# Second parts of split weights on VectorE, a ring of 2 MB slots for the second mixture, and a reordered chain in the first

## The chip, the cores and the metric

The kernel runs on one core of a Trainium2 chip as one program. The metric is the device time of one execution in microseconds; less is better. Four compute engines work side by side, each in its own order: TensorE (PE in the profile; its weight loads are PEld), VectorE (DVE), ScalarE (ACT) and GpSimd (POOL). SyncE (SP) issues most of the DMAs, which 16 DMA engines carry out.

## The reference

Two transformer blocks on 512 tokens of width 1024, in fp32. The first block: a mixer (mLSTM heads and a multi-scale pool), cross attention to a memory of 256 rows, and a mixture of 16 experts of width 256, two for each token. The second: a modulated Hyena convolution in its FFT form, and a mixture in which each of 16 experts of width 2048 chooses its 64 tokens. Cut to what matters here:

```python
z = x @ w_in                                   # mixer: q, k, v, o, u, gates
mixed = jnp.concatenate([h, pm], axis=-1); return mixed @ w_out
# first mixture: scores -> top 2 of the best group -> tokens by expert
hb = jax.nn.silu(xb @ w_gate[ei]) * (xb @ w_up[ei]); return hb @ w_down[ei]
# second mixture (expert choice): cap = 2 * 512 / 16 = 64
gate, idx = lax.top_k(jnp.swapaxes(aff, 1, 2), cap); xe = h[bidx, idx]
he = jax.nn.silu(xe @ w1) * (xe @ w3)
ye = (he @ w2) * gate; return zeros.at[idx].add(ye)
```

The weights of the second mixture are 402.65 MB, two thirds of all that the kernel reads.

## The kernel before

The stages follow each other: mixer and filters (two generators that are interleaved, so that TensorE alternates between them), output projection (`mix_out`), attention with the modulation vectors (`macc`), first mixture (`moe1`), its sum and layer norm (`combine`), the convolution (`hyena_first`, `hyena`, columns c of 256 or 512), the second router (`route2`) and the second mixture (`moe2`). A list scheduler sets each engine's order inside a stage; buffers come from pools whose slots rotate. The big pool has seven slots, the PSUM tags two or three buffers each.

A matmul of `mm` (lines 215 to 222) on operands of the class `Sp` is three matmuls in a shorter form, high x high, high x low and low x high (L218, L219, L220). `split` (L224) makes the parts: ScalarE copies the high one (L228), and another engine subtracts it to get the low one (L231), GpSimd unless the call names VectorE. `load_w` stages 512 KB of weights and splits them. The mixer's `proj` (L613) does not split: it multiplies x and the weights `wp` in full precision (L622, two instructions in the trace for each matmul). `wx` and `wh` are split weights, `mixl` the low part of the mixed rows, `fs` and `fk` operands of the filters, `fo` a sum of mirrored columns of the convolution (L1378), `ly` and `xr` steps of the layer norms (L308, L339, L340).

In `moe1` the logits (`plg`) go to scores, to the chosen experts (`mk`), to positions (`sv`); `lists(q)` compares the positions with 0 to 127 for four experts (`oh`, L1065), multiplies by token numbers and gates together (`pli`, L1070) and gives the index (`idx`) and the gates; `gather(e)` fetches the rows by an indirect DMA. Then for each expert: `columns` transposes the rows (`pt`, L1093) to `xe`, `up` gives `hb`, `turn` transposes it to `ht` (L1125 to L1127), and `down` multiplies by `wd` to `pye` and stores.

In `route2` VectorE finds the 64 largest of 512 by eight rounds (L1590), and `psv` turns the places. In `moe2`, `piece` issues a DMA of 1 MB (8 KB in each of 128 partitions) into one of 15 ring slots, with some of other shapes at the start. An expert takes 24 of them: `pa` and `pc` (L1682), `he`, the transposes `pht`, and `py` (L1724). Its 64 rows are multiplied by a row of the modulation (`yt`) and placed by `pcb` (L1737) with the matrix `ct`, whose 64 columns are the expert's gates, and added to `xr` (L1739). `pga` (L1661) is the gather of an expert's rows, done as a matmul.

Of the kernel before, what the change touches and what calls it, by code (L numbers as in the profile page):

```python
# [19 lines left out]
P = 128  # L20
S = 512
# [107 lines left out]
def layout(i):  # L129
# [45 lines left out]
    w1 = g["moe_w1_2"][0].reshape(E, 8, P, 4, 512).transpose(0, 3, 2, 1, 4)  # L175
    w3 = g["moe_w3_2"][0].reshape(E, 8, P, 4, 512).transpose(0, 3, 2, 1, 4)
    w13 = np.stack([w1[:, 0], w1[:, 1], w3[:, 0], w3[:, 1], w1[:, 2], w1[:, 3], w3[:, 2], w3[:, 3]], 1)
    o["w13"] = w13.reshape(E, 8, P, 2, 4, 512).transpose(0, 1, 3, 2, 4, 5)
    o["w2"] = g["moe_w2_2"][0].reshape(E, 8, 2, P, D).transpose(0, 1, 3, 2, 4)
# [24 lines left out]
class Builder:  # L204
# [379 lines left out]
    def mixer(self):  # L584
# [5 lines left out]
        x = self.big([P, 8, S], name="x")  # L590
        pg = self.psumt("pg")
        for h in range(4):
            nc.sync.dma_start(x[:, 2 * h:2 * h + 2], T["xT"][:, 2 * h:2 * h + 2])
            for k in (2 * h, 2 * h + 1):
                c = 32 * (k % 4)
                te.matmul(pg[c:c + 32], wg[:, k], x[:, k], start=k < 4, stop=k >= 4)
# [207 lines left out]
    def mix_out(self, xr, x1):  # L804

        m, mixed = self.bigsp([P, 8, S], "mix"), self.mixed
        for j in range(4):
            t = slice(j * P, (j + 1) * P)
            self.split(mixed[:, :, t], m[:, :, t], (self.nc.vector, self.nc.gpsimd)[j % 2])
# [147 lines left out]
    def moe1(self, xr, xT, xd):  # L957
# [17 lines left out]
        p = self.psumt("plg")  # L975
        for k in range(8):
            c = 32 * (k % 4)
            te.matmul(p[c:c + 32], rw[:, k], xT[:, k], start=k < 4, stop=k >= 4)
        ls = self.work(name="ls")
        act.activation(ls, p, AF.Copy)  # L980
        p = self.psumt("plt")[:, :64].rearrange("p (j e) -> p j e", e=E)
        for j in range(4):
            self.mm(p[:, j], ls[:, j * P:(j + 1) * P], sr)
        sc = sm([4, E], "sc")
        act.activation(sc, p, AF.Exp, scale=-1.0)
# [52 lines left out]
        wt = sm([4, E], "wt")  # L1038
        tt(wt, sc, mk, op=ALU.mult)
        vec.tensor_reduce(gx, wt, axis=AX.X, op=ALU.add)  # L1040
        vec.reciprocal(gx, gx)
        tt(wt, wt, gx[:, :, None].to_broadcast([P, 4, E]), op=ALU.mult)


        tg = sm([4, E, 5], "tg", BF16)
        for i in range(2):
            vec.tensor_copy(tg[:, :, :, i], row[:, :, i:i + 1].to_broadcast([P, 4, E]))
        gr = sm([4, E], "gr")
        for i in range(2, 5):
            vec.tensor_copy(tg[:, :, :, i], gr if i > 2 else wt)  # L1050
            if i < 4:
                tt(gr, gr if i > 2 else wt, tg[:, :, :, i], op=ALU.subtract)
# [8 lines left out]
        def lists(q, n=4):  # L1061
# [5 lines left out]
            p = self.psumt("pli")[:, :n * 5].rearrange("p (e c) -> p e c", c=5)  # L1067
# [3 lines left out]
            vec.tensor_reduce(idf[:, es], p[:, :, 0:2], axis=AX.X, op=ALU.add)  # L1071
            vec.tensor_copy(idx[:, es], idf[:, es])
            vec.tensor_reduce(gate[:, es], p[:, :, 2:5], axis=AX.X, op=ALU.add)
            return eq
# [22 lines left out]
        ready = lists(0)  # L1097
        for e in range(4):
            gather(e)
        cur = columns(0)  # L1100
        over = sm([4, E], "over")
# [65 lines left out]
        for e in range(E + 1):  # L1167
# [13 lines left out]
            if e < 3:  # L1181
                lists(4 * e + 4)
# [4 lines left out]
            if hb is not None:  # L1187
                down(e - 1, turn(hb))
# [313 lines left out]
    def route2(self, xr, z2, w):  # L1502
# [83 lines left out]

        m8 = self.C.tile([E, 8], F32, name="m8")
# [15 lines left out]
    def moe2(self, xr, hl, sv, aff):  # L1603
# [5 lines left out]
        m5 = self.W.tile([P, 512], F32, name="m5", tag="m5")  # L1609
# [14 lines left out]
        ring = [self.big([P, 2, 2048], name="ra") for _ in range(5)]  # L1624
        ring += [self.W.tile([P, 2, 2048], F32, name="r", tag="r", bufs=2) for _ in range(2)]
        ring = [t[:, i] for t in ring for i in range(2)]
        ring += [self.W.tile([P, 2048], F32, name="r1", tag="r1")]
        at = [0]

        spare = [self.W.tile([P, 2048], F32, name=f"s{i}", tag=f"s{i}") for i in range(2)]  # L1630
        hts = [self.W.tile([P, 1024], F32, name="ht", tag="ht"), spare[0][:, :1024]]
        xes = [self.W.tile([P, 512], F32, name="xe", tag="xe"), spare[0][:, 1024:1536]]
        cts, yts = ([spare[1][:, (2 * i + b) * 512:(2 * i + b + 1) * 512] for b in range(2)] for i in range(2))

        def piece(src, n=1):
            i, at[0] = at[0], at[0] + 1
            if i in (12, 15):

                n = 2 if i == 15 else 4
                t = [self.wide(name="r2") for _ in range(2)] if n == 2 else [m5] + [self.work(name="r4") for _ in range(3)]  # L1640
                t = [u.rearrange("p (a b) -> p a b", b=src.shape[2]) for u in t]
                h = src.shape[1] // n
                for i in range(n):
                    nc.sync.dma_start(t[i], src[:, i * h:(i + 1) * h])
                return lambda k: t[k // h][:, k % h]
            t = (ring[:13] + spare)[i] if i < 15 else ring[(i - 4) % len(ring)]
            t = t.rearrange("p (a b) -> p a b", b=src.shape[2])
            for i in range(n):
                c = slice(i * src.shape[1] // n, (i + 1) * src.shape[1] // n)
                nc.sync.dma_start(t[:, c], src[:, c])  # L1650
            return lambda k: t[:, k]

        def gather(e):
# [14 lines left out]
            xe = xes[e % 2].rearrange("p (h k s) -> p h k s", h=2, k=4)  # L1668
            act.activation(xe, pt.rearrange("p (k h s) -> p h k s", k=4, h=2), AF.Copy)
            return xe.rearrange("p h k s -> p (h k) s")  # L1670

        xs = gather(0)
        for e in range(E):
            ht = hts[e % 2].rearrange("p (k s) -> p k s", k=8)
            for hh in range(2):
                pa, pc = self.psum(name="pa"), self.psum(name="pc")
                for p, q in ((pa, 0), (pc, 2)):
                    for k2 in (0, 4):
                        w = [piece(T["w13"][e, 4 * hh + q + g, k2 // 4]) for g in range(2)]
# [94 lines left out]
```

## Time and profile before

| | |
|---|---|
| median of 3 runs (lowest, highest) | 2163.26 us (2154.15, 2169.12) |
| profiled execution | 2155.95 us |
| its span | 2154.2 us |
| TensorE busy | 1882.4 us (87%) |
| VectorE, ScalarE, GpSimd busy | 926.1, 510.3, 324.4 us |
| TensorE's mean granted clock | 0.951 |
| moved by DMA | 601.28 MB, mean 279 GB/s |

The span is the time from the first to the last instruction in the trace; 1.75 us of the profiled execution lie outside it. The granted clock is a share of 2.4 GHz: 1.00 is that level, and 0.50 is 1.2 GHz. Busy times are sums over stages that have different limits, so they are read stage by stage.

### The profile page before, as it was taken

How to read it: one execution, taken by the hardware profiler on the slowest of the kernel's cores; microseconds unless marked ns; L12 is line 12 of the kernel's file. 1: busy time of each engine (PE TensorE's matmuls, PEld its weight loads, DVE VectorE, ACT ScalarE, POOL GpSimd, SP SyncE). 2: the span in 40 equal slices, each digit the busy share in tenths (PEclk: the TensorE clock that was granted, in tenths of full speed). 3: DMA queues.
4: the chain of work that ended last, by engine and by line, in shares of the span. 5: the costliest groups of instructions: out<-in, count | busy, mean ns of one | idle time of the engine just before them, and what ended most of it. 6: DMA issues, size and time to landing. Idle time of an engine off the chain costs nothing.

```text
span 2154.2 us, 21248 instructions
## 1 busy us (share of the span) xinstructions
PE 1882.4 (87%) x8240; PEld 1009.2 (47%) x8240; DVE 926.1 (43%) x1340; ACT 510.3 (24%) x724; POOL 324.4 (15%) x208
## 2 busy tenths in 40 slices
PE   8999888989498877899786899998998888888996
PEld 2555567767265536787674233332333223332232
DVE  5666674575554548737998211111111110111113
ACT  4444223242255533443333100000000000000000
POOL 0000226310110024334653000000000000000001
PEclk9999998999699977999898899999999999999998
DMA  6443165673488861223246899999999999999995
GB/s 219 149 144 128 63 231 181 241 246 121 165 333 349 315 202 58 83 79 117 88 159 238 332 398 422 421 421 421 413 421 421 422 421 421 421 421 421 421 421 218
DMA packets 111715, 601.28 MB, mean 279 GB/s; under 512 B 14526, under 2 KB 16022, under 8 KB 58486
## 3 DMA queue, kind: packets, MB, share of 16 engines
q1 hardware_dynamic: 103478, 575.68, 68.1%
q0 software_dynamic: 3840, 13.31, 2.0%
q10 hardware_dynamic: 4288, 10.85, 1.3%
q8 instruction: 67, 1.10, 0.2%
q14 instruction: 42, 0.34, 0.1%
HBM read 577.74 MB, written 22.05 MB: 278 GB/s over the span
## 4 chain that ended last, share of the span: by engine, by line
PE 30%; DMA 19%; DVE 9%; issue 2%; POOL 1%; ACT 1%; DVEq 0%; SPq 0%; ACTq 0%; POOLq 0%
DMA ra<-in_w 12%; PE py L1724 8%; DMA r<-in_w 6%; PE pc L1682 5%; PE pa L1682 5%; PE pga L1661 2%; PE phy L218 2%; PE phy L219 1%; PE phy L220 1%; PE pcb L1737 1%; DVE wh L1415 1%; DVE fo L1378 1%; PE pht L1689 1%; DVE sp L1407 1%; DVE he L1686 1%
## 5 line engine op out<-in xcount | busy, mean ns | idle before, releaser
L1686 DVE TENSOR_TENSOR he<-he,pc 128x512 f32<-128x512 f32 x32 | 22.0, 688 | 479.7 <-PE pc L1682 452.4
L308 POOL TENSOR_TENSOR ly<-lve,mhalf 128x1 f32<-128x1 f32 x28 | 35.7, 1275 | 1068.2 <-DVE lve L320 1063.4
L231 POOL TENSOR_TENSOR wh<-w,wh 128x1024 fp32r<-128x1024 f32 x46 | 121.3, 2642 | 155.5 <-ACT wh L228 152.0
L1685 ACT ACTIVATE he<-pa 128x512 f32<-128x512 f32 x32 | 19.1, 597 | 474.8 <-PE pa L1682 468.3
L228 ACT ACTIVATE wh<-w 128x1024 fp32r<-128x1024 f32 x104 | 108.3, 1060 | 66.4 <-PE pb L220 13.7
L1727 DVE TENSOR_TENSOR s<-py,m 128x512 f32<-128x512 f32 x16 | 11.1, 691 | 227.4 <-PE py L1724 227.4
L1682 PE MATMUL pc<-ra,s 128*64 128x512 f32 x344 | 96.1, 596 | 11.6 <-DMA ra<-in_w 11.5
L1724 PE MATMUL py<-ra,ht 128*64 128x512 f32 x376 | 93.3, 595 | 0.0
L1682 PE MATMUL pc<-ra,xe 128*64 128x512 f32 x336 | 85.8, 594 | 6.6 <-DMA ra<-in_w 6.6
L1682 PE MATMUL pa<-ra,xe 128*64 128x512 f32 x336 | 86.6, 596 | 3.1 <-DMA ra<-in_w 2.4
L1682 PE MATMUL pa<-ra,s 128*64 128x512 f32 x336 | 86.1, 596 | 3.6 <-DMA ra<-in_w 3.6
L218 PE MATMUL phy<-hlh,wh 128*128 128x512 f32 (+1 forms) x240 | 87.5, 368 | 0.0
L219 PE MATMUL phy<-hll,wh 128*128 128x512 f32 (+1 forms) x240 | 86.5, 361 | 0.4 <-DVE hll L236 0.4
L220 PE MATMUL phy<-hlh,wh 128*128 128x512 f32 (+1 forms) x240 | 86.3, 360 | 0.0
L1737 PE MATMUL pcb<-s 64*128 64x512 f32 x256 | 67.7, 627 | 19.6 <-DVE s L1727 12.6
L1724 PE MATMUL py<-ra,s 128*64 128x512 f32 x312 | 81.2, 608 | 0.0
L222 PE MATMUL pye<-wd,ht 128*128 128x512 f32 x128 | 65.5, 659 | 17.3 <-ACT ht L1127 17.3
L858 DVE SCALAR_TENSOR_TENSOR macc<-wm,mc,macc 128x1024 f32<-128x1024 f32 x42 | 67.1, 1598 | 31.0 <-DMA wm<-in_modw 30.5
L1739 DVE TENSOR_TENSOR xr<-xr,pcb 128x1024 f32<-128x1024 f32 x60 | 70.6, 1218 | 20.0 <-PE pcb L1737 18.5
L231 DVE TENSOR_TENSOR wh<-w,wh 128x1024 fp32r<-128x1024 f32 x58 | 71.4, 1258 | 15.4 <-ACT wh L228 15.0
L1661 PE MATMUL pga<-hl,oh 128*64 128x512 f32 x256 | 60.3, 615 | 0.8 <-DVE oh L1656 0.8
L1682 PEld LDWEIGHTS pc<-ra,s 128*64 128x64 f32 x344 | 29.0, 137 | 65.6 <-issue 45.4
(532 smaller groups left out, 3925.7 us busy)
## 6 DMA issues: line engine op xcount, KB each, us to landing
ra<-in_w SPq DMA_DIRECT2D x254, 1024.0 KB
r<-in_w SPq DMA_DIRECT2D x125, 1024.0 KB
wm<-in_modw SPq DMA_DIRECT2D x48, 512.0 KB
w<-in_wgu SPq DMA_DIRECT2D x36, 512.0 KB
wd<-in_wd SPq DMA_DIRECT2D x16, 1024.0 KB
wg<-in_wgu SPq DMA_DIRECT2D x7, 2048.0 KB
wp<-in_wpair SPq DMA_DIRECT2D x10, 1024.0 KB
w<-in_wh SPq DMA_DIRECT2D x20, 512.0 KB
```

The source lines that it names most:

```text
L218: te.matmul(ps, a.h, b.h, start=first, stop=False, skip_group_check=skip)
L219: te.matmul(ps, a.h, b.l, start=False, stop=False, skip_group_check=skip)
L220: self.lastmm = te.matmul(ps, a.l, b.h, start=False, stop=last, skip_group_check=skip)
L222: te.matmul(ps, a, b, start=first, stop=last, skip_group_check=skip)
L228: nc.scalar.activation(d.h, f, AF.Copy)
L231: (lo_eng or nc.gpsimd).tensor_tensor(d.l, f, d.h.bitcast(F32), op=ALU.subtract)
L858: vec.scalar_tensor_tensor(acc, w, c[:, k:k + 1], acc, op0=ALU.mult, op1=ALU.add)
L1661: te.matmul(p[h * NS:(h + 1) * NS], oh[:, j], hl[:, j, h * 512:(h + 1) * 512], start=j == 0, stop=j == 3)
L1682: te.matmul(p[g * NS:(g + 1) * NS], xs[:, k2 + k], w[g](k), start=k2 + k == 0, stop=k2 + k == 7)
L1724: te.matmul(py[n * NS:(n + 1) * NS], ht[:, 4 * hh + 2 * (c % 2) + i, g * NS:(g + 1) * NS], w(i)[:, n * 512:(n + 1) * 512], start=c + i == ...
L1737: te.matmul(pb[n], ct[r, j * P:(j + 1) * P], yt[r], start=e < E - 1, stop=True)
L1739: tt(xr[:, j], xr[:, j], t.rearrange("p a b -> p (a b)"), op=ALU.add)
```

## The change

Seven edits in one.

- `split` takes VectorE where no engine is named, so the subtractions of the output projection, the attention and the convolution move there from GpSimd.
- The mixer splits x and its weights, and its projections use `mm`.
- `moe1`: the logits are made in tiles of 3 and 1 rows; `lists` multiplies by the token numbers alone, for one expert and then for three, and `weigh` makes the gates later; in the expert loop `turn` stands ahead of the next `columns`.
- `route2`: 14 matmuls on an unused PSUM tile (`pwarm`) stand after the last transposes.
- `moe2`: the weights lie in memory as pieces of 2 MB, 16 KB in each partition; `piece` fills eight slots in order, 12 pieces to an expert, and the ninth piece of all goes to other buffers by five smaller DMAs.
- `moe2`: the places of two experts are made at once (`places`); the rows of a pair stand in the two halves of the partitions, and `pcb` is done once for the pair with all 128 rows.
- There is one `ht` and one `xe` buffer, and the row of the modulation is loaded at full width.

```diff
-        (lo_eng or nc.gpsimd).tensor_tensor(d.l, f, d.h.bitcast(F32), op=ALU.subtract)
+        (lo_eng or nc.vector).tensor_tensor(d.l, f, d.h.bitcast(F32), op=ALU.subtract)
...
-        x = self.big([P, 8, S], name="x")
+        x = self.bigsp([P, 8, S], "x")
...
+            self.split(xf, x[:, 2 * h:2 * h + 2], vec)
...
-                nc.sync.dma_start(wp[0], T["wpair"][n])
+            w = self.load_w(T["wpair"][n, :, u], vec)
...
-                te.matmul(p, wp[0][:, u, k], x[:, k], start=k == 0, stop=k == 7)
+                self.mm(p, w[:, k], x[:, k], k == 0, k == 7)
...
+        for t in (slice(0, 3), slice(3, 4)):
+            n, c3 = (t.stop - t.start) * P, slice(t.start * P, t.stop * P)
+            p = self.psumt("plg")[:, :n]
...
-        ready = lists(0)
-        for e in range(4):
+        ready, oh0 = lists(0, 1)
+        gather(0)
+        _, oh1 = lists(1, 3)
+        for e in range(1, 4):
             gather(e)
         cur = columns(0)
+        wt = sm([4, E], "wt")
...
+        weigh(0, 1, oh0)
+        weigh(1, 3, oh1)
...
+            if hb is not None:
+                ht = turn(hb)
             if e + 1 < E:
                 cur = columns(e + 1)
...
-                down(e - 1, turn(hb))
+                down(e - 1, ht)
...
+        pw = self.psum(name="pwarm")
+        for i in range(14):
+            te.matmul(pw, self.ident, hl[:, 3, :512], start=True, stop=True)
...
+        slots = [self.big([P, 4096], name="ra") for _ in range(5)]
+        slots += [self.W.tile([P, 4096], F32, name="r", tag="r", bufs=3) for _ in range(3)]
...
+            t = slots[turn[0] % 8].rearrange("p (a b) -> p a b", b=1024)
+            turn[0] += 1
+            h = 4 // steps
+            for i in range(steps):
+                nc.sync.dma_start(t[:, i * h:(i + 1) * h], src[:, i * h:(i + 1) * h])
...
+            u = e % 2
+            if u == 0:
+                places(e)
...
+            for n in range(2):
+                o = (n ^ u) * NS
+                tt(yts[n][o:o + NS], py[o:o + NS], m5[o:o + NS, n * 512:(n + 1) * 512], op=ALU.mult)
+            if not u:
+                continue
```

TensorE at the start of the mixer, before: `pv` and `pqk` are projections, `psf` and `pgt` small matmuls of the filters and gates.

```order
L622 MATMUL pv<-x,wp 128x512 x8
L222 MATMUL psf<-sd,c_fw_113 64x512
L622 MATMUL pqk<-x,wp 128x512 x8
L655 MATMUL pgt<-c_ident,gn 128x64 x4
L622 MATMUL pqk<-x,wp 128x512 x4
```

The same place now:

```order
L218 MATMUL pv<-xh,wh 128x512
L219 MATMUL pv<-xl,wh 128x512
L218 MATMUL pqk<-xh,wh 128x512
L219 MATMUL pqk<-xl,wh 128x512
L222 MATMUL psf<-sd,c_fw_126 64x512
L220 MATMUL pv<-xh,wh 128x512
```

Each matmul of a projection has become three, and the first two projections are begun together.

TensorE where the first mixture's routing begins, before: the last products of attention's output, the last row's transposes, the logits.

```order
L219 MATMUL pb<-wh,oTh 128x512
L220 MATMUL pb<-wh,oTl 128x512
L360 MATMUL pt<-c_ident,xr 128x128 x8
L978 MATMUL plg<-x2T,c_rw 32x512 x8
L222 MATMUL plt<-c_sr,ls 128x16 x4
```

And now:

```order
L220 MATMUL pb<-wh,oTl 128x512
L360 MATMUL pt<-c_ident,xr 128x128 x8
L981 MATMUL plg<-x2T,c_rw 32x384 x8
L222 MATMUL plt<-c_sr,ls 128x16 x3
L981 MATMUL plg<-x2T,c_rw 32x128 x8
L222 MATMUL plt<-c_sr,ls 128x16
```

The logits of the first three tiles stand behind the transposes of the fourth, as the whole did.

ScalarE in the first mixture's expert loop, before: `wh` are copies of weights, `ye` is the scaled output.

```order
L1118 ACTIVATE hb<-pgu 128x256
L235 ACTIVATE xe<-pt 128x512
L1127 ACTIVATE ht<-pht_5578 128x256
L235 ACTIVATE xe<-pt 128x512
L1141 ACTIVATE ye<-pye,gate 128x1024
L1142 DMA yd<-ye 128x1024
L228 ACTIVATE wh<-wg 128x1024
```

And now:

```order
L1130 ACTIVATE hb<-pgu 128x256
L1139 ACTIVATE ht<-pht_5915 128x256
L235 ACTIVATE xe<-pt 128x512 x2
L1153 ACTIVATE ye<-pye,gate 128x1024
L1154 DMA yd<-ye 128x1024
L228 ACTIVATE wh<-wg 128x1024
```

The copy to `ht` has moved ahead of both copies to `xe`.

## Rows read from the trace of the kernel before

**Rows 1.** Windows: start:end, length, busy us by engine, PEclk, DMA share, GB/s

```profile
18.00:255.00 237.00, 230.04 (x740) 126.37 (x740) 153.73 (x267) 101.94 (x132) 23.90 (x36) 1.00 0.41 141
255.00:540.00 285.00, 254.01 (x1187) 194.78 (x1188) 180.35 (x210) 87.45 (x136) 87.87 (x39) 0.94 0.57 194
856.00:972.00 116.00, 105.44 (x514) 87.51 (x514) 61.15 (x107) 51.41 (x74) 41.70 (x17) 0.97 0.27 85
1228.00:1246.00 18.00, 17.16 (x85) 6.12 (x83) 1.80 (x3) 1.79 (x3) 0.00 (x0) 1.00 0.95 355
1446.00:2124.00 678.00, 611.87 (x2720) 207.02 (x2718) 98.59 (x143) 42.06 (x69) 0.00 (x0) 1.00 1.01 420
```

**Rows 2.** Timeline of TensorE in the mixer: start, us, engine, line, out<-in

```profile
26.61 7.13 PE L622 MATMUL pqk<-x,wp 128*128 128x512 f32 x16
...
60.92 0.39 PE L219 MATMUL pk<-fs,fk 128*128 128x512 f32 x1
...
62.55 0.39 PE L220 MATMUL pk<-fs,fk 128*128 128x512 f32 x1
```

**Rows 3.** Costliest groups: splits, busy us, mean ns | idle before

```profile
L228 ACT ACTIVATE wh<-w 128x1024 fp32r<-128x1024 f32 x104 | 108.3, 1060 | 66.4 <-PE pb L220 13.7
...
L231 DVE TENSOR_TENSOR wh<-w,wh 128x1024 fp32r<-128x1024 f32 x58 | 71.4, 1258 | 15.4 <-ACT wh L228 15.0
```

**Rows 4.** Groups of GpSimd from 255 to 540 us

```profile
L231 POOL TENSOR_TENSOR wh<-w,wh 128x1024 fp32r<-128x1024 f32 x24 | 63.4, 2647 | 63.4 <-ACT wh L228 63.3
...
L231 POOL TENSOR_TENSOR mixl<-mixed,mixh 128x1024 fp32r<-128x1024 f32 x2 | 5.7, 2888 | 6.6 <-ACT mixh L228 6.6
```

**Rows 5.** One line's instructions: ns min/median/max, first and last start

```profile
L858 DVE SCALAR_TENSOR_TENSOR macc<-wm,mc,macc x42: 1231/1285/3395, 295.6 to 489.3; 128x1024 f32<-128x1024 f32 x42
L1378 DVE TENSOR_TENSOR fo<-cv x8: 425/2466/2486, 854.7 to 900.4; 128x256 f32<-128x256 f32 x8
```

**Rows 6.** Waits of TensorE from 255 to 540 us: total, times, longest

```profile
PE pt L360 <- DVE xr L340: 10.8, 6, 3.8
...
PE pb L218 <- ACT wx L228: 5.5, 1, 5.5
PE pmd L866 <- DVE macc L858: 3.3, 3, 2.3
...
PE pb L219 <- DVE wx L231: 2.8, 1, 2.8
```

**Rows 7.** Timeline from 563 to 577 us

```profile
563.38 2.28 DVE L1065 TENSOR_TENSOR oh<-i128b,svb 128x2048 bf16<-128x2048 bf16 x1
567.73 0.59 PE L1070 MATMUL pli<-tg,oh 128*128 128x5 bf16 x16 [5.10 <-DVE tg L1050]
576.15 1.09 PE L1093 MATMUL pt<-c_ident,xg 128*128 128x128 f32 x4 [7.83 <-DMA xg<-xd,idx]
```

**Rows 8.** Waits of TensorE from 600 to 756 us

```profile
PE pye L222 <- ACT ht L1127: 14.8, 11, 4.3
```

**Rows 9.** Waits of TensorE from 856 to 972 us

```profile
PE pef L1325 <- DVE fo L1378: 8.8, 6, 2.0
```

**Rows 10.** Timeline of TensorE from 1190 to 1200 us

```profile
1192.10 0.73 PE L1599 MATMUL psv<-c_ident,at 16*128 16x16 f32 x4 [14.45 <-DVE at L1595]
1193.60 6.24 PE L1661 MATMUL pga<-hl,oh 128*64 128x512 f32 x16 [0.78 <-DVE oh L1656]
```

**Rows 11.** Window inside those gather matmuls

```profile
1196.00:1198.00 2.00, 2.00 (x8) 0.55 (x6) 0.00 (x0) 0.00 (x0) 0.00 (x0) 0.50 0.48 201
```

**Rows 12.** Chain that ended last: a later expert's gather

```profile
1633.04 3.43 PE pga L1661 x16
```

**Rows 13.** SyncE's queue, 1800 to 1900 and 692 to 696 us: packets, MB, share

```profile
q1 hardware_dynamic: 5771, 42.04, 101.1%
...
q1 hardware_dynamic: 84, 1.38, 80.2%
```

**Rows 14.** Timeline of TensorE from 2123 us

```profile
2123.08 9.17 PE L1724 MATMUL py<-ra,s 128*64 128x512 f32 x39
```

More of the change, by code (lines that the diff above doesn't have):

```diff
@@ L808, in mix_out @@
             t = slice(j * P, (j + 1) * P)
[L809 removed]
+            self.split(mixed[:, :, t], m[:, :, t])
         self.proj_ln(m, self.T["wmix"], xr, 0, x1)
@@ L973, in moe1 @@
         nc.sync.dma_start(yd[E * CAP:], zr)
[L975 to L983, printed above, removed]
-        sc = sm([4, E], "sc")
-        act.activation(sc, p, AF.Exp, scale=-1.0)
+        sc = sm([4, E], "sc")
+        for t in (slice(0, 3), slice(3, 4)):
+            n, c3 = (t.stop - t.start) * P, slice(t.start * P, t.stop * P)
+            p = self.psumt("plg")[:, :n]
+            for k in range(8):
+                c = 32 * (k % 4)
+                te.matmul(p[c:c + 32], rw[:, k], xT[:, k, c3], start=k < 4, stop=k >= 4)
+            ls = self.work(n, name="ls")
+            act.activation(ls, p, AF.Copy)
+            p = self.psumt("plt")[:, :64].rearrange("p (j e) -> p j e", e=E)
+            for j in range(t.start, t.stop):
+                self.mm(p[:, j], ls[:, (j - t.start) * P:(j - t.start + 1) * P], sr)
+            act.activation(sc[:, t], p[:, t], AF.Exp, scale=-1.0)
         vec.tensor_scalar(sc, sc, 1.0, None, op0=ALU.add)
@@ L1037, in moe1 @@
         vec.scalar_tensor_tensor(sv, p[:, :4], 1.0, mk, op0=ALU.add, op1=ALU.mult)
[L1038 to L1052, printed above, removed]
+        tr2 = sm([4, 2], "tr2", BF16)
+        vec.tensor_copy(tr2, row)
+        tg = sm([4, E, 3], "tg", BF16)
         idx, gate = sm([E], "idx", I32), sm([E], "gate")
@@ L1066, in lists, with weigh @@
                     svb[:, :, es, None].to_broadcast([P, 4, n, CAP]), op=ALU.is_equal)
-            p = self.psumt("pli")[:, :n * 5].rearrange("p (e c) -> p e c", c=5)
+            p = self.psumt("pli")[:, :n * 2].rearrange("p (e c) -> p e c", c=2)
+            for u in range(n):
+                for j in range(4):
+                    te.matmul(p[:, u], oh[:, j, u], tr2[:, j], start=j == 0, stop=j == 3)
+            vec.tensor_reduce(idf[:, es], p, axis=AX.X, op=ALU.add)
+            vec.tensor_copy(idx[:, es], idf[:, es])
+            return eq, oh
+        def weigh(q, n, oh):
+            p = self.psumt("plw")[:, :n * 3].rearrange("p (e c) -> p e c", c=3)
             for u in range(n):
@@ L1095, in columns @@
             return t
-        ready = lists(0)
-        for e in range(4):
+        ready, oh0 = lists(0, 1)
+        gather(0)
+        _, oh1 = lists(1, 3)
+        for e in range(1, 4):
             gather(e)
         cur = columns(0)
+        wt = sm([4, E], "wt")
+        tt(wt, sc, mk, op=ALU.mult)
+        vec.tensor_reduce(gx, wt, axis=AX.X, op=ALU.add)
+        vec.reciprocal(gx, gx)
+        tt(wt, wt, gx[:, :, None].to_broadcast([P, 4, E]), op=ALU.mult)
+        gr = sm([4, E], "gr")
+        for i in range(3):
+            vec.tensor_copy(tg[:, :, :, i], gr if i else wt)
+            if i < 2:
+                tt(gr, gr if i else wt, tg[:, :, :, i], op=ALU.subtract)
+        weigh(0, 1, oh0)
+        weigh(1, 3, oh1)
         over = sm([4, E], "over")
@@ L1632, in moe2 @@
[L1632 to L1651, printed above, removed]
+        slots = [self.big([P, 4096], name="ra") for _ in range(5)]
@@ new lines, in moe2, with piece @@
+        slots += [self.W.tile([P, 4096], F32, name="r", tag="r", bufs=3) for _ in range(3)]
+        turn = [0]
+        htb = self.W.tile([P, 1024], F32, name="ht", tag="ht")
+        xeb = self.W.tile([P, 512], F32, name="xe", tag="xe")
+        cts = [self.W.tile([P, 512], F32, name=f"ct{i}", tag=f"ct{i}") for i in range(2)]
+        yts = [self.W.tile([P, 512], F32, name=f"y{i}", tag=f"y{i}") for i in range(2)]
+        def piece(src, steps=1):
+            if turn[0] == len(slots) and slots[-1] is not None:
+                slots.append(None)
+                t = [self.wide(name="r4") for _ in range(2)] + [m5]
+                for k in range(3):
+                    nc.sync.dma_start(t[k], src[:, k])
+                t = [u[:, n * 512:(n + 1) * 512] for u in t for n in range(2)]
+                for n in range(2):
+                    t.append(yts[n])
+                    nc.sync.dma_start(yts[n], src[:, 3, n * 512:(n + 1) * 512])
+                return lambda k, n: t[2 * k + n]
+            t = slots[turn[0] % 8].rearrange("p (a b) -> p a b", b=1024)
[3 more added lines that the diff above has]
+                nc.sync.dma_start(t[:, i * h:(i + 1) * h], src[:, i * h:(i + 1) * h])
+            return lambda k, n: t[:, k, n * 512:(n + 1) * 512]
```

97 lines of the change are left out of this document (43 added, 54 removed).

## The prediction

> **What bounds the kernel now.** I read the busy time by stretch first, then in each stretch the waits of the engine that is nearest to full, then single instructions. From 18 to 255 us (mixer and filters) TensorE works 230 of 237 us at full clock, and no other engine is near: the end of this stretch is TensorE's sum of matmuls. From 255 to 540 us (output projection, attention) it idles 31 of 285 us while VectorE works 180. In the convolution from 856 to 972 us it idles 10.6 of 116. From 1446 to 2124 us the DMA engines are full at 420 GB/s, and TensorE waits for weights [rows 1]. So each microsecond saved ahead of that stream moves the stream's start, and the end with it, by as much; inside the stream only bytes and rate count.
>
> The profiled execution took 2155.95 us, 2154.2 of them in the span, 7.3 below the median of 2163.26. I sum against 2155.95 and add the 7.3 at the end.
>
> **The change part by part.**
>
> *Projections of the mixer.* A projection was 8 matmuls in full precision, 16 instructions in the trace, 7.13 us from first to last end, 16 x 0.43 = 6.9 us in a row of them. Now it is 24 matmuls of the split form. Seven of these start between 60.92 and 62.55, 0.233 us apart [rows 2], so a projection is 5.6 us: 1.3 saved, 26 us over 20 projections. All of it is on the path if the operands come in time. What it adds: 20 splits of weights and 4 of x, each an ACT copy and a VectorE subtraction of 1.26 us [rows 3]. That is 30 us, so VectorE's 154 of 237 become about 184 of some 218: cover for TensorE, but thin. x in two parts takes two slots, and the filters' operand fs has one buffer where it had two: each of eight fs then waits for the last matmul on the one before, plus about 1.06 (copy) and 1.22 (subtraction), 2.3 us, unless TensorE has a projection between; and the first projection waits for the splits of x, which I put at 3 us. If all eight gaps show, 18 + 3 of the 26 is lost. Range -26 to -5; I take **-16**, about the middle, since the order puts projections beside the filters' matmuls in some places only.
>
> *Output projection and attention.* 28 subtractions leave GpSimd: 24 of weights at 2.65 us, 2 of the mixed rows [rows 4] and 2 like them of the memory. On VectorE they cost 28 x 1.26 = 35 us. Beside a GpSimd split VectorE's own work stretches: a modulation step takes 1.285 us in the median and 3.395 at worst, the mean of the 42 is 1.598 [rows 5]; 42 x 0.31 = 13 us come back, and about 6 from the layer norms. So VectorE gets some 16 us more in a stretch where it has 105 free. What ends TensorE's waits there: the normed rows 10.8 us in six waits, the first weights of the projection 5.5 and 2.8 (behind mixed rows that GpSimd split), the modulation 3.3 [rows 6], 22.4 in all. A norm step at 1.28 for 3.4 takes about 2 from each of the longer waits, and the mixed rows' lower parts end sooner. I take **-9**, range 0 (the extra splits stand ahead of the norms on VectorE) to -16.
>
> *Routing of the first mixture.* The token lists no longer wait for the gates in three parts: the comparison of 2.28 us began at 563.38, but the list matmuls only at 567.73, after the last gate part, and the first gathered rows reached TensorE at 576.15 [rows 7]. Now the comparison is cut in 1 + 3 experts, both ahead of the index; 563.4 + 2.3 = 565.7 for 567.7. The gates move behind, where the first expert hides them. The order shows that the router's logits, cut in 3 + 1 tiles, still stand behind the last row's transposes, so this cut costs some 0.3 and gains nothing. **-2**, range 0 to -4.
>
> *Its expert loop.* TensorE waits 14.8 us in eleven waits for ht [rows 8]. In the new order ht stands ahead of xe on ScalarE (0.59 us), and all of the next expert's transposes stand ahead of the matmul that needs ht, so about 1.2 us come off each wait; three waits of over 2 us keep the rest, since hb still stands behind a copy that waits for the weights' DMA. Eleven waits, of which some are shorter than 1.2: **-7** with the copies of 1 us in the DMA's own gaps that follow it; range 0 to -12.
>
> *Second layer norms and convolution.* 22 subtractions go from GpSimd to VectorE. The sum fo takes 2.466 us in the median, 0.425 where no GpSimd split runs beside it [rows 5], and TensorE waits 8.8 us for it in six waits [rows 9]. VectorE gets 17 x 1.26 = 21 us in this stretch and gives back about 8 x 1.5 = 12, on 61 of 116 [rows 1]. So the 8.8 go; the norms before it gain a little as in attention. **-10**, range -4 to -14.
>
> *Warming matmuls in the second router.* TensorE rests 14.45 us up to 1192.10, and the first expert's gather matmuls then take 6.24 us [rows 10]; the granted clock in them is 0.50, the 1.2 GHz level [rows 11]. A later expert's take 3.43 [rows 12]. The 14 new matmuls are 28 instructions of 0.43 us, 12 us at 2.4 GHz and 24 at 1.2. At the low clock everything takes twice as long, so 6.24 for 3.43 means some 5 us at it before the clock rose; by that the new matmuls, which start at about 1177.7, end at about 1192, just when the top-k does. The gather takes 3.4 for 6.2: **-2.5**; if the clock stays low they end at 1202 and the next step waits 9.6 us.
>
> *The stream.* 402.65 MB of weights; pieces of 2 MB with rows of 16 KB for 1 MB with 8 KB, and 18.9 MB can be fetched ahead for 19.9, which costs 1.05 / 0.42 = 2.5 us. At 8 KB the stream had 42.04 MB in 101.1% of 100 us, 416 GB/s per busy time; the first mixture's gate weights, whose rows are 16 KB, had 1.38 MB in 80.2% of 4 us, 430 GB/s [rows 13]. That is 3%, from few packets; I take 2%, 420 to 429. (402.65 - 18.9) / 0.421 = 911 us become 894: **-17 + 2.5 = -14.5**, range +2.5 to -25. The Trainium skill, "DMA: Bandwidth & Descriptors", section "Why small descriptors are slow (HBM only)", speaks against so much: a fixed cost of about three cycles on a packet, beside one for each 32 bytes. By an estimate from that page, 8 KB to 16 KB would give 0.6%, 5 us, and the sum would be 12 us higher.
>
> *Tail.* The last 39 matmul instructions run to 2132.3 without a wait, 9.17 us [rows 14]; the last piece of weights is eight of them, 1.9 us, so TensorE is late there by an estimated 5 to 7. It is late because it places each expert's rows alone. Now pairs of experts are placed together, and expert 14 has no placing of its own (5 us), so TensorE is on time at the end: about -4.5, less 0.7 for a second multiplication and 1 for longer placing matmuls: **-3**, range -5 to +1.
>
> Sum: -16 - 9 - 2 - 7 - 10 - 2.5 - 14.5 - 3 = -64; 2155.95 - 64 = 2092, and 2099 on the scale of the median. I say **2100**.
>
> **The rivals.**
> 1. *VectorE becomes the bound* of the mixer and of attention. For it: 184 of 218 us, one fs buffer, more splits in front of the norms. Against: every added split belongs to a weight that is loaded early. The mixer then gives 5 and attention nothing: 2100 + 11 + 9 + about 5 for the norms of the convolution = 2125.
> 2. *The rate stays 421 GB/s.* For it: at 8 KB the share already reads 101%, and the 430 rests on 84 packets beside other queues. 2100 + 17 = 2117.
> 3. *A small packet cost, and nothing else, is saved*: 0.6% of the stream's 911 us is 5.5 us in place of 17, which gives 2112; this is what the page named above would have.
> 4. *The ring stalls*, the side of slower. A slot of 2 MB comes back only when eight steps have used it, in strict order. Before, while the ring was full in the first expert, 18 us went at 355 GB/s [rows 1]: 18 x 65 / 420 = 2.8 us lost. If coarse slots cost twice that in each of 16 experts, 90 us are added to 2100: 2190. It decides against the change from 64 / 16 = 4 us per expert. Against it: once TensorE waits for the DMA, most slots are empty, as in the stretch at 420 GB/s.
> 5. *The cut of the router's logits does what it is written for*, that is, its first three tiles run under the last row's norm and take 3 us of its wait: 2097. The order speaks against it.
>
> **How the numbers follow.** Forecast 0.60, with a range of its own of 2070 to 2128: the terms' deviations, 10, 8, 2, 6, 5, 5, 12 and 3 us, give 19 together if independent, and I take 1.5 of that. Rival 1: 0.14; rival 2: 0.13; rival 3: 0.05; rival 4: 0.04; rival 5: 0.04. Rivals 1 and 2 together would be at 2142, the upper end. Range 2068 to 2142. Over 1% (about what a measurement of this kernel can tell) faster is below 2141.6: all of the forecast and of rivals 2, 3 and 5, most of rival 1: 0.90. Within 1%: 0.06; slower: 0.04.
>
> **What would show it.** Mixer: its matmul work down by 26 us, the stretch that ended at 255 ending near 239, and waits of TensorE for fs below 10 us; above 18, rival 1 is right. Attention: modulation steps all near 1.285 and the waits for normed rows halved. Convolution: fo at 0.43 and no wait for it. Router: gather matmuls of 3.4 us, psv not behind the warming ones. Stream: over 425 GB/s between 1446 and 2040; at 421 rival 2, with dips to 350 in each expert rival 4. I am wrong above all if single-buffered fs leaves holes in a stretch that had none, or if the 430 GB/s of short bursts can't be held.

## The result, and the profile after

The changed kernel takes 2093.78 us in the median of four runs (2087.98 to 2096.50), the kernel before 2161.64 beside it: a ratio of 0.9683, 95% interval 0.9641 to 0.9724. The forecast was 2100 on the scale of 2163. The profiled execution of the changed kernel took 2096.14 us, 59.8 less than the 2155.95 of before.

Where these 59.8 us lie is read by cutting both traces at the first or last instruction of the same tile:

| stretch, and the instruction that ends it | before | after | difference | forecast |
|---|---|---|---|---|
| mixer and filters, to the first copy of mixed rows | 276.3 | 257.4 | -18.9 | -16 |
| output projection and attention, to the first logits | 276.0 | 258.8 | -17.2 | -9 |
| routing, to the first expert matmul | 25.6 | 24.9 | -0.7 | -2 |
| expert loop, to the last pye | 202.0 | 203.4 | +1.4 | -7 |
| sum and norms, then convolution, to the last phy | 206.6 | 196.9 | -9.7 | -10 |
| FFT steps and second router, to psv | 205.6 | 208.4 | +2.8 | 0 |
| psv and first gather, to the first pa | 9.8 | 8.9 | -0.9 | -2.5 |
| stream, to the last py | 929.8 | 912.3 | -17.5 | -17.5 with the tail |
| tail, to the end of the span | 22.5 | 23.4 | +0.9 | |

The same cut of the experiments below shows how far one execution can be trusted. The mixer is the same in ten of them, and its end lies between 257.0 and 266.3 us, with the trace after 261.6 in the mean, so its gain is 14.7 rather than 18.9. (Of the old form there are two traces, before and e2; both end at 276, with a clock of 1.00 in this window.) What shifts it is the granted clock early on, which these windows show, of the changed kernel and of experiment e8 (columns as in [rows 1]):

```profile
24.00:100.00 76.00, 72.83 (x310) 53.03 (x309) 65.11 (x107) 49.57 (x62) 4.84 (x5) 1.00 0.41 140
```

```profile
24.00:100.00 76.00, 71.73 (x288) 52.02 (x287) 59.71 (x95) 48.37 (x60) 4.84 (x5) 0.94 0.39 129
```

The column of the granted clock (PEclk) reads 1.00 and 0.94: with about the same busy time, fewer instructions are done. All eleven traces follow it: at 1.00 the mixer ends at 257.0 and 257.4 us, at 0.93 at 265.9 and 266.3, the others in between. The attention, from the same cuts of seven other runs with its code, takes 251 to 257 us, 255 in the mean: a gain of 21.

The windows of the changed kernel, for [rows 1], in its own stretches:

```profile
23.30:257.40 234.10, 223.84 (x961) 167.40 (x960) 188.56 (x316) 122.42 (x154) 24.02 (x40) 0.99 0.43 143
257.40:516.20 258.80, 233.78 (x1152) 182.39 (x1152) 176.76 (x217) 90.69 (x138) 12.81 (x9) 0.96 0.62 212
541.10:744.50 203.40, 177.09 (x776) 119.70 (x776) 104.45 (x126) 103.59 (x140) 16.20 (x18) 0.95 0.83 308
782.50:940.90 158.40, 151.47 (x798) 129.14 (x798) 95.67 (x170) 68.70 (x95) 5.83 (x4) 0.95 0.27 86
1400.00:2065.00 665.00, 597.94 (x2620) 206.88 (x2618) 85.40 (x166) 42.06 (x69) 0.00 (x0) 0.99 1.00 426
```

The third column of times is VectorE: it does 189 of 234 us in the mixer. In attention it does 177, hardly more than the 172 which it did before between the same marks, although 28 subtractions came to it. GpSimd has gone from 88 to 13 us there. The attention before, between these marks:

```profile
276.30:552.30 276.00, 240.51 (x1153) 187.87 (x1153) 171.50 (x187) 89.72 (x138) 87.91 (x37) 0.93 0.58 197
```

Not all of the gain is waiting that went away. TensorE's busy time for the same matmuls fell from 240.5 to 233.8 us, with the granted clock at 0.93 and then 0.96; its idle time fell from 35.5 to 25.0.

The projections run as forecast; matmuls of one in the timeline of TensorE, for [rows 2], six intervals of 0.233 us:

```profile
60.03 0.40 PE L220 MATMUL pv<-xh,wh 128*128 128x512 f32 x1
...
61.43 0.39 PE L220 MATMUL pv<-xh,wh 128*128 128x512 f32 x1
```

The modulation step and fo, one line each with the shortest, median and longest in ns, for [rows 5]:

```profile
L858 DVE SCALAR_TENSOR_TENSOR macc<-wm,mc,macc x42: 1264/1283/1287, 278.1 to 453.7; 128x1024 f32<-128x1024 f32 x42
L1392 DVE TENSOR_TENSOR fo<-cv x8: 417/422/426, 816.8 to 853.3; 128x256 f32<-128x256 f32 x8
```

No long ones are left: the largest are 1.287 and 0.426 us, for 3.395 and 2.486.

TensorE's waits from 257 to 516 us, for [rows 6]:

```profile
PE pt L360 <- DVE xr L340: 7.1, 4, 6.1
PE ppt L936 <- DVE pe L931: 7.0, 5, 2.8
PE pb L218 <- ACT wx L228: 5.7, 1, 5.7
```

Of the 7.1 for the normed rows, 6.1 is one wait at the end, ahead of the first mixture, which stood outside the stretch of [rows 6]; of the 10.8 there about 1 is left. Of the 3.3 for the modulation 0.2 is left. The wait of ScalarE's copy of wx stayed.

The queue of the stream from 1800 to 1900 us, for [rows 13] (packets, MB, share):

```profile
q1 hardware_dynamic: 2931, 42.68, 100.4%
```

Half the packets, and 42.68 MB for 42.04 in the same 100 us.

In the convolution one wait for fo is left, where [rows 9] has six:

```profile
PE pef L1339 <- DVE fo L1392: 2.8, 1, 2.8
```

### The profile page after: what moved, and what is told of

It reads as the page before. It is cut to its first block, busy times and chain, and to the rows that moved or that the text cites. A ratio compares the mean times of both kernels' runs of the same rounds, so it can differ in the third digit from the quotient of the medians.

```text
span 2094.4 us, 21241 instructions
## 1 busy us (share of the span) xinstructions
PE 1854.0 (89%) x8380; PEld 1043.7 (50%) x8380; DVE 944.2 (45%) x1465; ACT 536.8 (26%) x752; POOL 186.3 (9%) x157
## 4 chain that ended last, share of the span: by engine, by line
PE 41%; DMA 16%; DVE 8%; issue 3%; ACT 2%; POOL 2%; DVEq 0%; SPq 0%; ACTq 0%; POOLq 0%
PE py L1747 11%; DMA ra<-in_w 8%; PE pc L1713 6%; PE pa L1713 6%; DMA r<-in_w 5%; PE pga L1678 3%; DMA wg<-in_wgu 2%; PE pye L222 2%; PE pcb L1764 2%; PE phy L218 2%; PE phy L220 2%; PE phy L219 2%; POOL ly L308 1%; DVE lst L316 1%; DVE wh L231 1%
## 5 line engine op out<-in xcount | busy, mean ns | idle before, releaser
L1713 PE MATMUL pa<-ra,xe 128*64 128x512 f32 x768 | 178.5, 595 | 9.1 <-DMA ra<-in_w 8.5
L231 DVE TENSOR_TENSOR wh<-w,wh 128x1024 fp32r<-128x1024 f32 x124 | 151.4, 1237 | 36.3 <-ACT wh L228 34.9
L1747 PE MATMUL py<-ra,ht 128*64 128x512 f32 x640 | 150.3, 599 | 0.0
L1713 PE MATMUL pc<-r,xe 128*64 128x512 f32 x512 | 119.0, 602 | 16.9 <-DMA r<-in_w 16.9
L1713 PEld LDWEIGHTS pa<-ra,xe 128*64 128x64 f32 x768 | 58.5, 137 | 115.3 <-issue 94.0
L1747 PE MATMUL py<-r,ht 128*64 128x512 f32 x376 | 92.1, 595 | 0.7 <-DMA r<-in_w 0.7
L1747 PEld LDWEIGHTS py<-ra,ht 128*64 128x64 f32 x640 | 47.7, 138 | 90.2 <-issue 89.9
L1713 PEld LDWEIGHTS pc<-r,xe 128*64 128x64 f32 x512 | 38.6, 138 | 94.2 <-issue 74.0
L222 PE MATMUL pye<-wd,ht 128*128 128x512 f32 x128 | 60.9, 618 | 11.3 <-ACT ht L1139 11.3
L1764 PE MATMUL pcb<-y,ct 128*128 128x512 f32 x128 | 57.2, 598 | 6.5 <-DVE y L1753 6.5
L1423 POOL TENSOR_TENSOR sp<-sp,sp 128x512 f32<-128x512 f32 x32 | 46.8, 1482 | 175.8 <-DVE sp L1422 175.6
```

The source lines that it names most:

```text
L222: te.matmul(ps, a, b, start=first, stop=last, skip_group_check=skip)
L231: (lo_eng or nc.vector).tensor_tensor(d.l, f, d.h.bitcast(F32), op=ALU.subtract)
L1423: pool.tensor_tensor(t[2 * i], t[2 * i], t[2 * i + 1], op=op)
L1713: te.matmul(p[g * NS:(g + 1) * NS], xs[:, 4 * kh + k], w(k, g), start=kh + k == 0, stop=kh + k == 4)
L1747: te.matmul(py[o:o + NS], ht[:, 4 * hh + i, g * NS:(g + 1) * NS], w(i, n), start=c + i == 0, stop=c + i == 6)
L1764: te.matmul(pb[n], cts[n][:, j * P:(j + 1) * P], yts[n], start=e < E - 1, stop=True)
```

## The experiments

All start from the changed kernel; times are medians, ratios are to the kernel before on the same chip.

**e1: the default of split back on GpSimd.**

```diff
-        (lo_eng or nc.vector).tensor_tensor(d.l, ...)
+        (lo_eng or nc.gpsimd).tensor_tensor(d.l, ...)
...
-            self.split(mixed[:, :, t], m[:, :, t])
+            self.split(mixed[:, :, t], m[:, :, t], (self.nc.vector, self.nc.gpsimd)[j % 2])
```

> The changed kernel with the default of split set back to GpSimd and the mixed rows split in turn by VectorE and GpSimd. Theory: the subtractions beside VectorE's work are what attention and convolution lost, so the 17 us of attention and the 10 us of the convolution come back: 2093.8 + 27 = about 2121, the modulation step has a maximum of 3.4 us again and fo 2.47 in the median. Rival: most of the gain there comes from the earlier rows of the mixer and from the clock, not from the engine of the subtractions; then the time rises by less than 12 us, to at most 2106.

2128.69 us, ratio 0.9869 (0.9828 to 0.9911): 35 above the changed kernel, more than the 27 of the theory and far from the rival. Between the marks of the table attention takes 280.1 us and the convolution's stretch with the norms 210.2. The same two lines and the window of attention, of this run:

```profile
L858 DVE SCALAR_TENSOR_TENSOR macc<-wm,mc,macc x42: 1230/1285/3405, 284.2 to 481.1; 128x1024 f32<-128x1024 f32 x42
L1392 DVE TENSOR_TENSOR fo<-cv x8: 426/2466/2628, 838.3 to 885.1; 128x256 f32<-128x256 f32 x8
```

```profile
263.50:543.60 280.10, 242.00 (x1155) 188.95 (x1156) 169.53 (x189) 90.15 (x138) 86.36 (x37) 0.93 0.58 196
```

TensorE's busy time there is back too: 242.0 us at a granted clock of 0.93.

**e2: the mixer's projections in full precision again.**

```diff
-        x = self.bigsp([P, 8, S], "x")
+        x = self.big([P, 8, S], name="x")
...
-            w = self.load_w(T["wpair"][n, :, u], vec)
+                wp[0] = self.W.tile([P, 2, 8, P], F32, name="wp", tag="wh", bufs=3)
+                nc.sync.dma_start(wp[0], T["wpair"][n])
...
-                self.mm(p, w[:, k], x[:, k], k == 0, k == 7)
+                te.matmul(p, wp[0][:, u, k], x[:, k], start=k == 0, stop=k == 7)
```

> The changed kernel with the mixer's projections in full precision on weights that are not split, as before. Theory: TensorE's sum alone sets the end of this stretch, so the 19 us that the trace shows there come back, 2113, with TensorE's busy time in the stretch up by 26. Rival: VectorE, which then has 30 us less to do in the stretch, was slowing the filters, and the old form gains part of it back: 2106 or less.

2106.93 us, ratio 0.9765 (0.9725 to 0.9805): 13 above, just over the bound that was set for the rival. The trace does not bear the rival out, though: the mixer ends at 276.1 us, as before the change, so nothing of the old form was gained back. The 19 of the theory came from one execution with a fast start; against the mean of 261.6 the mixer is worth 14.5.

**e3: rows of 8 KB.** Each slot is filled by two DMAs of 1 MB.

```diff
+            steps = max(steps, 2)
             h = 4 // steps
```

> The changed kernel with each piece of 2 MB fetched by two DMAs of 1 MB, whose rows are 8 KB; slots, their order and the arithmetic stay. Theory: the longer rows alone raise the rate, so it falls from 427 to 421 GB/s and the end comes 900 x 1.4% = 13 us later, 2107. Rival (a small fixed cost for a packet, 0.6%): 5 us, 2099. Rival (the ordered ring or fewer copies of rows made the stream faster): no change, 2094.

2106.48 us, ratio 0.9761 (0.9721 to 0.9801): 12.7 above, as the theory has it. The window of the stream in this run:

```profile
1400.00:2065.00 665.00, 600.97 (x2588) 196.25 (x2584) 84.72 (x165) 42.05 (x69) 0.00 (x0) 0.99 1.01 420
```

420 GB/s for 426, and the stretch from the first pa to the last py takes 924.7 us for 912.3, and for 911.1 to 911.5 in the other runs. The queue from 1800 to 1900 us is that of before to the packet:

```profile
q1 hardware_dynamic: 5771, 42.03, 101.1%
```

Shorter rows here also mean twice as many DMAs. The packets in the traces tell the two apart: from 1800 to 1900 us one of 8 KB takes 314 ns in the mean, in this run and before, and one of 16 KB 616 ns, 2% less than two of 8 KB. The packets of 4 bytes, 16 to a DMA, fill 0.4% of the DMA engines' time with 8 KB and 0.2% with 16 KB. So most of it is the row.

**e4: the loop's old order.**

```diff
-            if hb is not None:
-                ht = turn(hb)
...
-                down(e - 1, ht)
+                down(e - 1, turn(hb))
```

> The changed kernel with the transposes to ht behind the next expert's columns again, as before. Theory: the loop of the first mixture is bound by its weights, and a wait taken from ht comes back as a wait for weights, so the time stays within 3 us of 2093.8 though the waits for ht rise from 11 to about 17 us. Rival (the prediction's own step): 7 us more, 2101.

2092.94 us, ratio 0.9705 (0.9664 to 0.9745): no difference from the changed kernel that can be told. The loop takes 205.8 us between the marks, and TensorE waits 19.4 us for ht in it, against 11.3. A wait of 8 us more made the loop 2 us longer than in the profile after, and 3 longer than in the mean of the eight runs with the new order (197.7 to 205.5, 202.4 in the mean), just outside their spread.

```profile
PE pye L222 <- ACT ht L1139: 19.4, 15, 3.7
```

**e5: GpSimd's work put back beside VectorE's.**

```diff
+        if lo_eng is None:
+            nc.gpsimd.tensor_tensor(f, f, d.h.bitcast(F32), op=ALU.subtract)
```

> The changed kernel, in which GpSimd makes each moved subtraction a second time, in place in the staged weights, after VectorE has made it; nothing waits for its result but the next load into that buffer. Theory: what the change took away is GpSimd's work beside VectorE's (VectorE's instructions stretched to 3.4 us, and the small step of the norms queued behind it on GpSimd); then attention and convolution lose most of their 27 us again, 2112 to 2121. Rival: it was the 2.65 us of a GpSimd subtraction in the path of TensorE's operands; then the time stays below 2100, since VectorE still delivers.

2160.87 us, ratio 1.0015 (0.9995 to 1.0034): 67 above, as much as the change's whole gain, and more than twice what the theory expected. The rival falls as an account of the whole: no operand of TensorE comes from GpSimd here, and attention still takes 300.7 us, 46 more than the 255 of the mean; the stretch of norms and convolution takes 217.7 for 196.9. TensorE's waits in attention:

```profile
PE pt L362 <- DVE xr L342: 19.7, 7, 6.1
PE ppt L938 <- DVE pe L933: 14.5, 7, 3.2
PE pb L219 <- DVE wx L231: 7.6, 2, 7.2
```

What waits is what VectorE makes: normed rows 19.7 us for 7.1, softmax rows 14.5 for 7.0. TensorE's busy time is up too, 247.7 us at a granted clock of 0.90:

```profile
264.00:564.70 300.70, 247.66 (x1156) 192.34 (x1158) 220.89 (x217) 90.31 (x138) 103.54 (x39) 0.90 0.53 183
```

The size beyond e1 has two sources that this run does not part: VectorE's own subtractions now run beside GpSimd's (its total is 220.9 us for 176.8), and a staged buffer comes free only when GpSimd has been through it. The second is there: SyncE, which issues the loads, waits 39.9 us in ten waits for GpSimd to be through with a buffer.

**e6: the last weights of the first mixture left out for 14 experts.**

```diff
-                fetch_down(e)
+                if e < 2:
+                    fetch_down(e)
```

> The changed kernel without the loads of the first mixture's last weights for experts 2 to 15: 14 MB less, those experts use the weights of experts 0 and 1. Theory: the loop waits for weights, so it shortens towards TensorE's own 177 us, from 203 to 185 or less. Rival: the chain from hb over ht to pye bounds it; then it stays above 198.

A single run, 2079.63 us. The loop takes 193.2 us, between the two bounds, so neither holds alone: 14.7 MB fewer are some 35 us of the DMA engines at 420 GB/s, and gave 10. The waits for ht fall to 5.2 us.

**e7: no warming matmuls** (the 14 matmuls taken out).

> The changed kernel without the 14 warming matmuls. Theory from the trace: they gave 0.9 us (the gather took 5.35 us for 6.24, at a granted clock of 0.72 for 0.50), so 2094.7, no change that can be told. Rival (the prediction's 2.5 us): 2096. Nothing below 2093 if they cost nothing.

2090.98 us, ratio 0.9692 (0.9652 to 0.9731): the run cannot tell them from nothing. In the trace the step from psv to the first pa takes 9.9 us without them; with them it takes 8.8 or 8.9 in five of the runs and 7.1 or 7.2 in six, so they give 1 to 2.8 us.

**e8: the logits in a free PSUM tag.**

```diff
-            p = self.psumt("plg")[:, :n]
+            p = self.psum(name="plg")[:, :n]
```

TensorE in the changed kernel's order and here, with - and +:

```
 L219 MATMUL pb<-wh,oTh 128x512
 L220 MATMUL pb<-wh,oTl 128x512
+L981 MATMUL plg<-x2T,c_rw 32x384 x8
 L360 MATMUL pt<-c_ident,xr 128x128 x8
-L981 MATMUL plg<-x2T,c_rw 32x384 x8
 L222 MATMUL plt<-c_sr,ls 128x16 x3
```

> The changed kernel with the router's logits in another PSUM tag, which is free there; the order then puts the logits of three tiles ahead of the last row's transposes. Theory: the cut gave nothing because its PSUM buffer came last; now 2 us of the chain to the first expert go, 2092. Rival: the chain waits for the last row's norm and the scores anyway, no change at all.

2084.75 us, ratio 0.9658 (0.9621 to 0.9696): 9 below the changed kernel by the medians, which come from different chips, 5 by the ratios, and the intervals overlap. From the first matmul of attention's last product to the first expert matmul it takes 87.7 us for 91.2, but in the ten runs with the changed kernel's code there it lies between 87.4 and 91.4. So a gain is likely and not shown by this run alone.

**e9: the copies of the gate weights behind ht.** From the profile after: these rows of the timeline are ScalarE and TensorE in the middle of the loop.

```profile
617.18 1.06 ACT L228 ACTIVATE wh<-wg 128x1024 fp32r<-128x1024 f32 x1 [8.88 <-DMA wg<-in_wgu]
618.14 0.37 ACT L1130 ACTIVATE hb<-pgu 128x256 f32<-128x256 f32 x1
618.40 0.38 ACT L1139 ACTIVATE ht<-pht 128x256 f32<-128x256 f32 x1
...
618.83 5.37 PE L222 MATMUL pye<-wd,ht 128*128 128x512 f32 x8 [5.14 <-ACT ht L1139]
...
624.23 0.33 SPq L1145 DMA_DIRECT2D wd<-in_wd  x1
```

ScalarE stands 8.88 us at a copy whose weights have not landed; hb and ht, 0.37 and 0.38 us of work, are queued behind it, and TensorE waits 5.14 us for ht. SyncE issues the next fetch of wd at 624.23, as pye ends.

```diff
-                with tc.issue_after(after[4 * e + i > 2].ins) if e < 2 else nullcontext():
+                with (tc.issue_after(after[4 * e + i > 2].ins) if e < 2 else
+                      tc.issue_after(hts[-1].ins) if e > 2 and big else nullcontext()):
...
-            act.activation(ht, pt[:, :256], AF.Copy)
+            hts.append(act.activation(ht, pt[:, :256], AF.Copy))
```

> The changed kernel with ScalarE's copies of the first mixture's gate weights (the ones that come by 2 MB) issued behind the last ht. Theory: what is left of the waits for ht (11.3 us in eight, the longest 5.1) is a copy that waits for the weights' DMA ahead of hb and ht on ScalarE, and while pye waits SyncE can't fetch the next expert's last weights; with the order turned round both go, and the loop shortens from 203 by 8 us or more. Rival: the copies, late now, hold TensorE back by as much, and the loop stays at 200 to 204 us.

2079.50 us, ratio 0.9633 (0.9613 to 0.9653), beside 2090.75 of the changed kernel on the same chip (e11). The loop takes 190.6 us. TensorE's wait for ht, in the changed kernel and here:

```profile
PE pye L222 <- ACT ht L1139: 11.3, 8, 5.1
```

```profile
PE pye L222 <- ACT ht L1142: 3.3, 4, 1.3
...
ACT wh L228 <- DMA wg<-in_wgu: 4.4, 3, 2.2
```

ScalarE itself waits 4.4 us for these weights; in the changed kernel it was

```profile
ACT wh L228 <- DMA wg<-in_wgu: 20.4, 5, 8.9
```

**e10: e8 and e9 together, and e11: the changed kernel again.**

> The logits in their own PSUM tag and the copies behind ht, together. If the two earlier edits are worth 3 and 8 us: 11 below the changed kernel of the same job. If neither is: no difference beyond 4 us.

2075.60 us, ratio 0.9607 (0.9584 to 0.9631): the fastest of all, 15 below the changed kernel on the same chip, the 11 of the theory and a little more, and below both kernels.

> The changed kernel itself, for the comparison with the two others on the same chip. Theory on its spread: the mixer's end lies at 257 or at 266 us, by the granted clock of the first 100 us alone, so the times spread over some 9 us; 2085 to 2097.

2090.75 us (2084.73 to 2095.76), ratio 0.9673 (0.9651 to 0.9695): the spread is as expected. Its mixer ends at 259.1 us, at neither of the two places that were named; over all traces the ends lie between them, with the clock.

## Why the prediction was right, and where its terms were off

The time was forecast within 7 us, and most of the rows on which it rests came out. Two terms were off by more than 5 us, the attention and the expert loop, and cancelled each other, so that the sum is as close as it is has a share of luck. (The deviations listed for the range give 20 us together, not 19; the range hardly changes.)

**Mixer, -16: 14.7 in the mean, and e2 gives 13.** TensorE's busy time between the marks fell from 249.8 to 223.8 us in the profile, the 26 that were worked out, and to 226.8 in the mean of the eleven traces. What was taken off stands elsewhere than supposed: the first projection begins 4.7 us later (23.3 for 18.6; 3 were put down), and the waits for fs stayed at 2.2 us (2.5 before), so the single buffer cost nothing that shows. The rest is the clock of the first 100 us in most runs. Rival 1 (VectorE becomes the bound) did not happen, with VectorE busy 189 of 234 us, more than the 184 of the sum.

**Attention, -9: some 21 in the mean, 17 in the profile.** The step that failed is the price put on GpSimd's company: the sum took 2 us off each of the longer waits for normed rows, and let VectorE be 16 us busier. In fact those waits vanish nearly whole, and VectorE's total hardly rises, since what it got back (42 modulation steps at 1.281 for 1.598 us, norms at 1.28 for 1.54 and 1.80) covers some 20 of the 35, and VectorE's other instructions 10 more. And the sum had no term for TensorE's own work: some 7 of the 21 are its busy time, 240.5 us before and 233.0 in the mean of the seven runs, at granted clocks of 0.93 and of 0.96 or 0.97. e1 shows that the engine of the subtractions is the cause, e5 that GpSimd's work beside VectorE's costs as much and more when TensorE uses none of its results, though in e5 the loads also stand behind it. How much of it is stretched instructions and how much the small step of the norms (ly) that queues behind a subtraction on GpSimd stays open; VectorE stood 5.5 us for that step before and 1.8 after.

**Routing, -2: 0.7 in the profile, 1.9 in the mean.** The ten runs with this code take 22.1 to 25.2 us, 23.7 in the mean, for the 25.6 of the one trace before. The order left the cut of the logits without a gain, and e8, which gave them their own buffer, doesn't settle it. The parts of this term were not run apart.

**Expert loop, -7: nothing.** The step that failed is the one from "about 1.2 us come off each wait" to as much off the loop. Some of it came off: 17.3 us of waits for ht before,

```profile
PE pye L222 <- ACT ht L1127: 17.3, 14, 4.3
```

became 11.3 (e4 has 19.4 with the old order and the changed kernel's other edits), but the loop takes 202.4 us in the mean of the eight runs with the new order, for 202.0. By e4 the order alone gives between nothing and 3 us. The forecast named the copy that waits for the weights' DMA, and treated it as a rest on three waits only. It is what holds the loop: while it holds ht, it holds pye and with it the next fetch. e9, which moves such copies alone, takes 12 us out of the loop. That a wait saved elsewhere comes back at this copy is the reading that fits e4 and e9; no run follows a single wait. e6 shows that fewer bytes do part of the same.

**Norms and convolution, -10: 9.7**, and e1 gives it back. fo went to 0.422 us, but its waits gave 6.0 of the 8.8 that were put down. The rest comes from two other waits for VectorE that are gone, and for which the sum had no term: 5.1 us for the low part of the normed rows (hll) and 1.9 for z. In e1 both are back, 5.6 and 1.9.

**Warming, -2.5: 0.9 in the profile, 1 to 2.8 in all.** The matmuls end before the top-k, 13.4 us after their start for the 14 that were worked out; the granted clock was at 0.50 in the first 2 us of them, where the working took 5. It does not hold, see below. psv does not stand behind them.

**Stream and tail, -17.5: 16.6.** The rate is 426 to 427 GB/s, between the 421 of rival 2 and the 429 that was taken, and e3 shows that pieces in rows of 16 KB are worth 12 to 14 us, not the 17 of the sum. The rest, 5 us, is that TensorE follows the last weights more closely, which the sum had in its tail: from the first pa to the landing of the last weights, by the packets in the traces, it takes 921.6 us before, 922.8 in e3 and 910.2 in the changed kernel. So the stream by itself gave 11 for the 14.5 of the sum. The 0.6% of rival 3, by the Trainium skill's fixed cost of a packet ("DMA: Bandwidth & Descriptors", "Why small descriptors are slow (HBM only)"), is too little: the measured share is 1.4%. Rival 4 did not happen. In windows of 10 us counted from the first pa, the kernel before falls to 354 to 407 GB/s in five of those between 20 and 70 us, and the changed one and e3 in none; what is left is the first window (198 for 202) and one about 300 us later (399 for 375). The tail was to be shorter, since TensorE would be nearly on time, and it is: TensorE's last py ended 8.7 us after the last weights landed before (2132.3 and 2123.6), and 2.7 after now (2071.6 and 2068.9; 2.5 to 2.7 in all runs). From that landing to the end of the span it takes 25.5 us for 30.7, so the tail gave 5 for the 3 that were put down; the marks of the table count most of it to the stream. The last matmuls run without a wait in both; in the timeline of the changed kernel:

```profile
2064.52 7.09 PE L1747 MATMUL py<-r,ht 128*64 128x512 f32 x32 [0.65 <-DMA r<-in_w]
```

7.1 us in a row, for 9.2 in [rows 14]. That it is the pairs that brought TensorE up was not run apart.

**FFT and second router, 0: +2.8 in the profile**, from -0.2 to +5.1 in the other runs; none of the edits was meant for it. The traces point to what is left of VectorE and GpSimd side by side. In the changed kernel GpSimd begins a step on `rows` just ahead of a product on zc, and VectorE takes 3.43 us for that product:

```profile
1068.68 2.89 POOL L1529 TENSOR_TENSOR rows<-rows 128x1024 f32<-128x1024 f32 x1 [12.35 <-DMA rows<-in_lnr]
1069.23 3.43 DVE L1487 TENSOR_TENSOR zc<-zc,x 128x1024 f32<-128x1024 f32 x1
```

In e4 VectorE comes first, by 0.2 us, and takes 1.22:

```profile
1066.19 1.22 DVE L1485 TENSOR_TENSOR zc<-zc,x 128x1024 f32<-128x1024 f32 x1
1066.39 3.28 POOL L1527 TENSOR_TENSOR rows<-rows 128x1024 f32<-128x1024 f32 x1 [13.26 <-DMA rows<-in_lnr]
```

All thirteen traces divide so: with 1.2 us for that product (before, e4, e8, e10) the stretch takes 205.4 to 206.7 us, with 3.4 it takes 208.4 to 210.7. No run moves this step alone.

## What to carry to other kernels

Before sharing elementwise work between VectorE and GpSimd, compare the longest and the median duration of the same VectorE instruction: two clear values (1.28 and 3.4 us here) say what the sharing costs, and taking GpSimd out can leave VectorE hardly busier (177 us for 172 in attention, with 28 subtractions more). A wait that is shortened counts only if it is the one that holds the loop: look first for an in-order engine that stands at a transfer with short work queued behind it, since the two instructions after the copy cost 0.75 us here, and getting them out from behind it gave 12. And with the DMA engines full, longer rows still gave 1.4% of the rate here (16 KB for 8 KB), while every microsecond ahead of the stream still counts in full.

## What was not expected of the hardware

TensorE's granted clock came up in the warming matmuls and went down again under the gather that they were meant for. The timeline and the windows of the changed kernel:

```profile
1135.17 13.41 PE L1603 MATMUL pwarm<-hl,c_ident 128*128 128x512 f32 x28
1149.83 0.63 PE L1617 MATMUL psv<-c_ident,at 16*128 16x16 f32 x4 [1.24 <-DVE at L1613]
1151.23 5.35 PE L1678 MATMUL pga<-hl,oh 128*64 128x512 f32 x16 [0.78 <-DVE oh L1673]
```

```profile
1148.00:1151.00 3.00, 1.17 (x6) 0.39 (x4) 2.51 (x6) 0.00 (x0) 0.00 (x0) 1.00 0.74 296
1151.00:1156.00 5.00, 4.77 (x16) 1.45 (x16) 0.51 (x2) 0.00 (x0) 0.00 (x0) 0.66 0.17 61
```

The gather took 5.35 us, with a mean granted clock of 0.66 in it, so part of it at 1.2 and part at 2.4 GHz; it follows on 2.6 us in which TensorE did only four small transposes. In six runs of eleven with the same matmuls this fall did not come, and the step was 1.7 us shorter.

And GpSimd's subtractions, made once more for nobody (e5), cost 67 us in 2094; how much of that is the loads that stood behind them isn't known.
